# Attention stages tied in one order on the tensor engine, value products behind the transposes, and linear-attention products grouped by rows and columns

## The chip, the cores and the metric

The kernel runs on one core of a Trainium2 chip. The metric is the device time of one execution in microseconds (us), as a median of runs; a profiled execution gives the times of the single instructions. The engines are TensorE (PE in the rows, PEld for its weight loads), VectorE (DVE), ScalarE (ACT), GpSimd (POOL) and SyncE (SP), which issues most DMAs. Each engine runs its own list of instructions in the order in which the program was built, and waits at semaphores for the others.

## What is computed

One inference step of a two-layer diffusion backbone, on 512 latent tokens and 128 context tokens. Layer 0 mixes neighbourhood attention and a bidirectional gated linear attention, layer 1 is grouped-query attention; a convolutional feed-forward block follows each. Cut to what the change touches:

```
def block_attention(q, k, v):                 # layer 1, and context tokens of layer 0
    s = einsum('bhgqd,bhkd->bhgqk', qblk, k) * scale
    p = softmax(s, axis=-1)
    return einsum('bhgqk,bhkd->bhgqd', p, v)

def neighbourhood_attention(...):             # layer 0, latent tokens
    s_loc = q . k_window * scale + bias;  s_ctx = q . k_ctx * scale
    p = softmax(concat([s_loc, s_ctx], -1))
    o = p[..., :nk] . v_window + p[..., nk:] . v_ctx

def gla_scan(q, k, v, g, s0):                 # layer 0, linear attention, forward and backward
    o_inter = (q * exp(bcum)) . s             # from the running state
    att[i, j] = sum_d q[i,d] k[j,d] decay(i, j, d)
    o = o_inter + att . v
    s_new = exp(blast) * s + k_dec^T . v
```

## The kernel before, in words

Activations lie with features on the partitions and the 640 tokens (NT) along the free dimension, in two halves of 320. Projections split each operand into a high and a low part in float32r and take three matmuls per 128 x 128 block (`step`, L153); in the rows these are `mm`, each 128 rows by 128 columns of the array and 320 columns of moving data.

An attention is cut into units. A unit of layer 1 is one head and one block of 128 queries: its stage `scores` makes four matmuls into PSUM (`gs`, L1259 and L1260); `exps` takes the row maximum (L1011) and multiplies it by the scale (L1013) on VectorE, and the exponential with its row sum on ScalarE (L1017); `norm` takes the reciprocal of the sum (L1022) and scales the probabilities `gp` by it on VectorE (L1025); `turn` transposes these in five blocks of 128 on TensorE (`gpt`, L1268); `gather` copies them to SBUF (`gpy`, L1272 on VectorE, L1273 on ScalarE); `values` multiplies by the values for two heads at once (`gpo`, L1279: ten matmuls of 128 rows by 64 columns, the two heads in the two column halves). Layer 0's units have the same stages (`nas`, `nap`, `napt`, `napx`, `napo`), with a bias added to the scores. After each head pair comes a unit for the context tokens (`ctxs`, `ctxpt`, `ctxo`).

`pipeline` traces the stages of three successive units in turn: scores and exps of the newest, gather and values of the oldest, norm and turn of the middle one. Behind each stage it draws a few steps of other work (`fill.some(rate)`: in layer 1 the query projections of later heads and the first half of the output projection). Stages are traced at a higher priority (`AHEAD`) than the fill, and a scheduler then orders each engine's list at build time by priority and readiness. `tc.issue_after(ins)` makes what is traced under it follow `ins` on the same engine. In layer 1 (`paced`) the fill has to follow the last stage that returned an instruction, which is `scores` only, since no other stage returns one.

The linear attention (`gla_scores`, `gla_states`, `gla_out`) builds, for two head pairs m, products of 32 x 32 (`lev`, L860), of 32 and 64 columns (`off`, L881 and L884), and the outputs (`go`: the product with the values at L949 on all 128 rows, two products with the states, forward L951 and backward L952, on the 64 rows of one head). A matmul with float32 operands shows as two records in the trace; a transpose shows as one.

Of the kernel before, what the change touches and what calls it, by code (L numbers as in the profile page):

```python
# [18 lines left out]
LAT = 512  # L19
CTX = 128  # L20
NT = LAT + CTX
# [9 lines left out]
def kernel(ctx: ExitStack, tc: tile.TileContext, a: dict, o: dict):  # L31
    nc = tc.nc
# [799 lines left out]
    def gla_scores(m, k, q, F, G, fill):  # L832
# [38 lines left out]
        fill.some(ROFF, SOFF)  # L871
        big, small = PS("off"), PS("offx")
        res = {}
        for e in range(2):
            pe = slice(64 * e, 64 * e + 64)
            for t in range(5):
                dst = big[:, e, 128 * t:128 * t + 128] if t < 4 else small[:, e, 0:128]
                for j in range(4):
                    b = j // 2
                    s = slice(128 * t + 32 * j, 128 * t + 32 * j + 32)  # L880
                    nc.tensor.matmul(dst[32 * j:32 * j + 32, 64 * b:64 * b + 64], A32[pe, s],  # L881
                                     B32[pe, 128 * t + 64 * b:128 * t + 64 * b + 64], start=True, stop=True)
# [53 lines left out]
    def gla_out(m, q, F, G, vg, att, S, OT, fill):  # L936
        qd = []
        for c in (F, G):
            x = C("qd")
            last = expo(x[:, 0:NT], c[:, 0:NT])  # L940
            nc.gpsimd.tensor_tensor(x[:, 0:NT], x[:, 0:NT], q[:, 0:NT], ALU.mult)
            qd.append(x)
        for e, pe in col_pairs():
            h = 2 * m + e
            ps = PS("go")
            for t in range(5):
                dst = ps[:, 0, 128 * t:128 * t + 128] if t < 4 else ps[:, 1, 0:128]
                s = slice(128 * t, 128 * t + 128)
# [81 lines left out]
    def na_units(m, q, kk, kl, kch, kcl, vw, vc, vctx, ot):  # L1030
        units = []

        def unit(bp, e, mates):
# [20 lines left out]
            def turn():  # L1054
                u["pt"] = [P1("napt") for _ in range(2)]
                for i in range(2):
                    for t in range(3):
                        nc.tensor.transpose(u["pt"][i][:, 128 * t:128 * t + 128], u["p"][i][:, 128 * t:128 * t + 128], ident)

            def gather():  # L1060
                u["x"] = [T("napx", "napx", n=512, bufs=4) for _ in range(2)]
# [6 lines left out]
            def values():  # L1068
                po = P1("napo", "po")
                for i in range(2):  # L1070
                    b = 2 * bp + i
                    for t in range(3):
                        v = vw[b, t] if t < 2 else vc
                        for f in range(2):
                            hh = 2 * m + f
                            nc.tensor.matmul(po[64 * f:64 * f + 64, 128 * i:128 * i + 128], v[:, 64 * hh:64 * hh + 64],  # L1076
                                             mates[f]["x"][i][:, 128 * t:128 * t + 128], start=(t == 0), stop=(t == 2))
                dst = ot[:, 0:LAT].rearrange("p (r b i) -> p b r i", b=4, i=16)
                nc.scalar.copy(dst[:, 2 * bp:2 * bp + 2], po[:, 0:256].rearrange("p (b r i) -> p b r i", b=2, i=16))

            u.update(scores=scores, turn=turn, gather=gather)
            if e:
# [10 lines left out]
    def context_unit(q, kk, kl, ks, scale, vcol, ot):  # L1093
        u = {}

        def scores():
            ps = PS("ctxs")
            for e in range(2):
                dst = ps[:, e, 0:128]
                nc.tensor.matmul(dst, q[e][:, LAT:NT], kk[e][:, ks], start=True, stop=False)  # L1100
                nc.tensor.matmul(dst, q[e][:, LAT:NT], kl[e][:, ks], start=False, stop=True)
            u["s"] = ps[:, :, 0:128]

        def turn():
            u["pt"] = P1("ctxpt")
            for e in range(2):
                nc.tensor.transpose(u["pt"][:, 128 * e:128 * e + 128], u["p"][e], ident)

        def gather():
            u["x"] = T("ctxx", "ctxx", n=256, bufs=1)  # L1110
# [2 lines left out]
        def values():  # L1113
            po = P1("ctxo", "po")
            for e in range(2):
                nc.tensor.matmul(po[64 * e:64 * e + 64, 0:128], vcol(e), u["x"][:, 128 * e:128 * e + 128], start=True, stop=True)
            nc.scalar.copy(ot[:, LAT:NT], po[:, 0:128])

        def view():
            t = T("ctxp", "ctxp", n=256, bufs=2)  # L1120
# [32 lines left out]
    def layer1(xs, rs, mods):  # L1153
# [91 lines left out]
        def units_of(m, q, r):  # L1245
# [5 lines left out]
            def unit(b, e, mates):  # L1251
# [23 lines left out]
                def values():  # L1275
                    po = P1("gpo", "po")
                    for t in range(5):
                        for f in range(2):
                            nc.tensor.matmul(po[64 * f:64 * f + 64, 0:128], vs[t][:, 64 * kv:64 * kv + 64],  # L1279
                                             mates[f]["x"][:, 128 * t:128 * t + 128], start=(t == 0), stop=(t == 4))  # L1280
                    nc.scalar.copy(ot[:, s], po[:, 0:128])

                u.update(scores=scores, turn=turn, gather=gather)
                if e:
# [308 lines left out]
```

## Time and profile before

| | |
|---|---|
| median of 3 runs | 1748.98 us (1746.35 to 1754.0) |
| profiled execution: device time | 1748.81 us |
| profiled execution: span from the first to the last instruction | 1747.0 us |
| TensorE busy | 1672.7 us, 96% |
| VectorE busy | 1277.5 us, 73% |
| ScalarE busy | 722.8 us, 41% |
| chain that ended last: share of TensorE / VectorE / DMA | 81% / 12% / 3% |

How to read it: a busy TensorE is a union of spans whose ends are modelled, and matmuls overlap, so what an instruction costs is read from the distance between the starts of successive rows, not from its duration. The linear attention lies between 90 and 282 us, the neighbourhood attention to 420, the grouped-query attention between 983 and 1225; the rest is projections and the feed-forward blocks.

### The profile page before, as it was taken

To read this page: it belongs to the slowest core of one execution; us is meant where nothing else is said; L and a number is where in the kernel's file an instruction comes from. 1 tells how busy PE (TensorE), PEld (TensorE's weight loads), DVE (VectorE), ACT (ScalarE), POOL (GpSimd) and SP (SyncE) were. 2 spreads that over 40 slices of the span, in tenths; PEclk is the share of its full clock that TensorE was granted. 3 is DMA by queue.
4 is the path that set the end of the run, shared out by engine and by line. 5 is a ranking of instruction groups with operands and counts; after the bars stand their busy time and mean duration, and the time that the engine had idled before them with its cause. 6 is when DMAs were issued, how large, how long until landed. Compare 5 with 4: busy or idle time off the path is not lost.

```text
span 1747.0 us, 33431 instructions
## 1 busy us (share of the span) xinstructions
PE 1672.7 (96%) x13142; PEld 1573.8 (90%) x13142; DVE 1277.5 (73%) x2877; ACT 722.8 (41%) x1599; POOL 206.2 (12%) x475
## 2 busy tenths in 40 slices
PE   8978899989999999999999999999999999999997
PEld 6867777879899999999998788878899999999997
DVE  5899954765899989997557988875775644663654
ACT  4443254454533322332335566754453322331342
POOL 2134441310200000000003311000110000000001
PEclk8988998999999999999999999999999999999998
DMA  8623223233154555444232200110212222222222
GB/s 314 207 91 130 98 86 99 80 101 97 55 175 155 159 169 183 148 149 131 69 120 89 66 20 19 35 67 22 73 61 74 85 73 73 73 66 93 72 64 72
DMA packets 68014, 175.22 MB, mean 100 GB/s; under 512 B 7920, under 2 KB 9744, under 8 KB 66832
## 3 DMA queue, kind: packets, MB, share of 16 engines
q1 hardware_dynamic: 67024, 171.48, 30.2%
q8 instruction: 103, 1.69, 0.4%
q0 software_dynamic: 832, 1.60, 0.3%
q14 instruction: 55, 0.45, 0.1%
HBM read 165.71 MB, written 7.34 MB: 99 GB/s over the span
## 4 chain that ended last, share of the span: by engine, by line
PE 81%; DVE 12%; DMA 3%; ACT 2%; issue 2%; POOL 0%; SPq 0%; ACTq 0%; DVEq 0%; POOLq 0%
PE mm L153 65%; PE gpo L1279 3%; PE gpt L1268 2%; DVE junk L316 1%; DVE wa L316 1%; PE gs L1259 1%; DMA wa<-in_ada_wt_dram 1%; DVE wl L112 1%; PE gs L1260 1%; PE napo L1076 1%; DVE eb L847 1%; PE ss L410 1%; PE go L949 1%; DVE ea L841 1%; DMA x<-in_xT_dram 1%
## 5 line engine op out<-in xcount | busy, mean ns | idle before, releaser
L153 PE MATMUL mm<-hh,wl 128*128 128x320 f32 x2080 | 651.7, 315 | 5.3 <-DVE x L488 1.0
L153 PE MATMUL mm<-hl,wh 128*128 128x320 f32 x2080 | 648.4, 312 | 0.0
L153 PE MATMUL mm<-hh,wh 128*128 128x320 f32 x2080 | 642.0, 312 | 0.0
L111 ACT CAST wh<-ws 128x512 fp32r<-128x512 f32 x376 | 228.8, 615 | 443.0 <-PE mm L153 404.0
L153 PEld LDWEIGHTS mm<-hh,wl 128*128 128x128 f32 x2080 | 394.6, 190 | 15.6 <-issue 5.9
L153 PEld LDWEIGHTS mm<-hl,wh 128*128 128x128 f32 x2080 | 395.4, 190 | 2.9 <-DVE h L445 1.2
L153 PEld LDWEIGHTS mm<-hh,wh 128*128 128x128 f32 x2080 | 393.3, 190 | 0.9 <-issue 0.3
L112 DVE TENSOR_TENSOR wl<-ws,wh 128x512 fp32r<-128x512 f32 x348 | 240.2, 693 | 159.3 <-ACT wh L111 158.4
L153 PE MATMUL mm<-glo,wh 128*128 128x320 f32 x704 | 217.0, 309 | 0.0
L153 PE MATMUL mm<-ghi,wh 128*128 128x320 f32 x704 | 216.7, 309 | 0.0
L153 PE MATMUL mm<-ghi,wl 128*128 128x320 f32 x704 | 215.8, 309 | 0.0
L488 DVE SCALAR_TENSOR_TENSOR x<-mm,mod,x 128x192 f32<-128x192 f32 (+2 forms) x240 | 96.8, 435 | 93.4 <-PE mm L153 92.6
L153 PEld LDWEIGHTS mm<-ghi,wl 128*128 128x128 f32 x704 | 131.7, 188 | 0.9 <-issue 0.9
L153 PEld LDWEIGHTS mm<-glo,wh 128*128 128x128 f32 x704 | 132.2, 188 | 0.0
L153 PEld LDWEIGHTS mm<-ghi,wh 128*128 128x128 f32 x704 | 132.0, 188 | 0.1
L316 DVE SCALAR_TENSOR_TENSOR junk<-wa,sb 128x512 f32<-128x512 f32 x160 | 115.6, 727 | 7.5 <-DMA wa<-in_ada_wt_dram 7.2
L316 DVE SCALAR_TENSOR_TENSOR wa<-wa,sb 128x512 f32<-128x512 f32 x160 | 117.7, 742 | 0.3
L522 POOL MEMSET u<- 128x1 f32 x88 | 8.9, 103 | 766.3 <-DVE gate L515 432.3
L525 ACT COPY u<-mm 128x320 f32<-128x320 f32 x88 | 37.8, 432 | 88.0 <-PE mm L153 83.1
L592 PE MATMUL tm<-wl,hh 128*128 128x256 f32 x200 | 58.6, 297 | 9.8 <-ACT v L601 7.0
L1011 DVE TENSOR_REDUCE mx<-gs 128x1 f32<-128x640 f32 x64 | 52.5, 821 | 16.6 <-PE gs L1260 16.0
L1017 ACT ACTIVATE gp<-gs,mx,rq 128x640 f32<-128x640 f32 x64 | 57.1, 892 | 9.5 <-DVE mx L1013 5.1
(302 smaller groups left out, 2480.7 us busy)
## 6 DMA issues: line engine op xcount, KB each, us to landing
ws<-in_wu_dram SPq DMA_DIRECT2D x88, 512.0 KB, 3.2
wa<-in_ada_wt_dram SPq DMA_DIRECT2D x160, 256.0 KB, 3.3
ws<-in_wd_dram SPq DMA_DIRECT2D x32, 448.0 KB, 3.2
aw<-in_ada_w_dram SPq DMA_DIRECT2D x8, 1024.0 KB, 15.7
ws<-in_w_ab_dram SPq DMA_DIRECT2D x16, 512.0 KB, 4.2
ws<-in_wd_dram SPq DMA_DIRECT2D x16, 512.0 KB, 3.7
x<-in_xT_dram SPq DMA_DIRECT2D x16, 320.0 KB, 5.5
ws<-in_w_gqa_dram SPq DMA_DIRECT2D x10, 512.0 KB, 3.9
```

The costliest lines, as they stand in the source:

```text
L111: nc.scalar.copy(hi, src)
L112: eng.tensor_tensor(lo, src, hi, ALU.subtract)
L153: nc.tensor.matmul(ps, x, y[:, s], start=st, stop=sp_)
L316: nc.vector.scalar_tensor_tensor(w if v else junk, w, 1.0, cs[v, j], ALU.mult, ALU.mult, accum_out=acc[:, k, v, j:j + 1])
L410: nc.tensor.matmul(ps[0:rows, c:c + 2], part[:, t], onesd, start=True, stop=True)
L488: nc.vector.scalar_tensor_tensor(x[:, b:e], ps[:, b - HN * h:e - HN * h], gate[:, v, m:m + 1], old[:, b:e], ALU.mult, ALU.add)
L525: nc.scalar.copy(u[:, 1:321], ps)
L592: nc.tensor.matmul(ps, hh[:, s], wlo, start=(k == 0), stop=False)
L1011: nc.vector.tensor_reduce(mx[:, 0:n], s, axis, ALU.max, negate=True)
L1017: nc.scalar.activation(dst, src, AF.Exp, bias=mx[:, i:i + 1], accum_out=sm[:, i:i + 1], **kw)
L1268: nc.tensor.transpose(dst, u["p"][0][:, 128 * t:128 * t + 128], ident)
L1279: nc.tensor.matmul(po[64 * f:64 * f + 64, 0:128], vs[t][:, 64 * kv:64 * kv + 64], mates[f]["x"][:, 128 * t:128 * t + 128], start=(t == 0), ...
```

## The change

Four edits. `pipeline` puts `values` behind `norm` and `turn`, and makes each stage's TensorE instructions follow the last one of the stage before it (`behind_it`); every stage with TensorE work now returns its last instruction. The fill of layer 1 is paced by scores and values, not by turn. In `gla_scores` the `off` products of 32 columns all come before those of 64 columns. In `gla_out` the products with the values come first for the five token blocks, then the products with the states. Line numbers of the code behind the change are about 15 higher.

```diff
@@ gla_scores
-        for e in range(2):
-            pe = slice(64 * e, 64 * e + 64)
-            for t in range(5):
-                dst = big[:, e, 128 * t:128 * t + 128] if t < 4 else small[:, e, 0:128]
-                for j in range(4):
-                    ...
-                    nc.tensor.matmul(dst[32 * j:32 * j + 32, 64 * b:64 * b + 64], A32[pe, s],
+        blocks = [(e, slice(64 * e, 64 * e + 64), t, big[:, e, 128 * t:128 * t + 128] if t < 4 else small[:, e, 0:128])
+                  for e in range(2) for t in range(5)]
+        for width in (32, 64):
+            for e, pe, t, dst in blocks:
+                if width == 32:
+                    for j in range(4):
+                        ...
+                    continue
                 for b in range(2):
                     nc.tensor.matmul(dst[64 * b:64 * b + 64, 64 - 64 * b:128 - 64 * b],
@@ gla_out
             for t in range(5):
-                nc.tensor.matmul(dst, vg[t][:, 128 * h:128 * h + 128], att[m, e][:, s], start=True, stop=(t == 4))
-                if t < 4:
-                    nc.tensor.matmul(dst, S[m, 0][pe, t, :], qd[0][pe, s], start=False, stop=False)
-                    nc.tensor.matmul(dst, S[m, 1][pe, 3 - t, :], qd[1][pe, s], start=False, stop=True)
+                nc.tensor.matmul(dst[t], vg[t][:, 128 * h:128 * h + 128], att[m, e][:, cols[t]], start=(t in (0, 4)), stop=(t == 4), skip_group_check=True)
+            for t in range(4):
+                nc.tensor.matmul(dst[t], S[m, 0][pe, t, :], qd[0][pe, cols[t]], start=False, stop=False, skip_group_check=True)
+                nc.tensor.matmul(dst[t], S[m, 1][pe, 3 - t, :], qd[1][pe, cols[t]], start=False, stop=(t == 3), skip_group_check=True)
@@ pipeline
+        behind_it = None
...
-            for lag, stage in ((0, "scores"), (0, "exps"), (2, "gather"), (2, "values"), (1, "norm"), (1, "turn")):
+            for lag, stage in ((0, "scores"), (0, "exps"), (2, "gather"), (1, "norm"), (1, "turn"), (2, "values")):
                 if stage in window[lag]:
-                    with tc.high_priority(offset=AHEAD):
+                    with tc.high_priority(offset=AHEAD), ExitStack() as behind:
+                        if behind_it is not None:
+                            behind.enter_context(tc.issue_after(behind_it))
                         last = window[lag][stage]()
                     if last is not None:
-                        fill.after = last.ins
+                        behind_it = last.ins
+                        if stage != "turn":
+                            fill.after = last.ins
@@ turn, values of the three kinds of unit, scores of the context unit
-                        nc.tensor.transpose(dst, u["p"][0][:, 128 * t:128 * t + 128], ident)
+                        last = nc.tensor.transpose(dst, u["p"][0][:, 128 * t:128 * t + 128], ident)
+                    return last
```

In layer 1 of the program before, TensorE's list mixes transposes of one unit with value products of others; this piece is the one that ran from 1139.10 us.

```order
L1279 MATMUL gpo<-gpy,v 64x128
L1268 MATMUL gpt<-ident,gp 128x128 x2
L1279 MATMUL gpo<-gpy,v 64x128
L1268 MATMUL gpt<-ident,gp 128x128
L1279 MATMUL gpo<-gpy,v 64x128
L1268 MATMUL gpt<-ident,gp 128x128
L1279 MATMUL gpo<-gpy,v 64x128
L1268 MATMUL gpt<-ident,gp 128x128
L1279 MATMUL gpo<-gpy,v 64x128 x4
L1279 MATMUL gpo<-gpy,gvc 64x128 x2
L1259 MATMUL gs<-gkk,q 128x320
```

The same engine and layer in the changed program, an unbroken piece of its list, shows each stage whole.

```order
L1274 MATMUL gs<-gkl,q 128x320
L153 MATMUL mm<-hh,wl 128x320
L153 MATMUL mm<-hl,wh 128x320
L153 MATMUL mm<-hh,wh 128x320
L153 MATMUL mm<-hh,wl 128x320
L153 MATMUL mm<-hl,wh 128x320
L153 MATMUL mm<-hh,wh 128x320
L1282 MATMUL gpt<-ident,gp 128x128 x5
L1294 MATMUL gpo<-gpy,v 64x128 x8
L1294 MATMUL gpo<-gpy,gvc 64x128 x2
L1273 MATMUL gs<-gkk,q 128x320
```

The value products have moved together behind the five transposes; between the scores of a unit and the transposes of the unit before it stand six matmuls of fill here.

VectorE's list of the changed program at such a place, with buffer numbers: the maximum of one unit's scores (mx_13090), the normalisation that belongs to it (gp_13092), and between them the maximum of the next unit's scores (gs_13114).

```order
L1020 TENSOR_REDUCE mx_13090<-gs_13085 128x1
L1022 TENSOR_TENSOR mx_13090<-mx_13090,rq_10745 128x1
L1287 COPY gpy_13128<-gpt_13107 128x256
L112 TENSOR_TENSOR wl_13948<-ws_13945,wh_13947 128x512
L1020 TENSOR_REDUCE mx_13119<-gs_13114 128x1
L1031 RECIPROCAL sm_13091<-sm_13091 128x1
L1022 TENSOR_TENSOR mx_13119<-mx_13119,rq_10745 128x1
L1034 TENSOR_SCALAR gp_13092<-gp_13092,sm_13091 128x640
```

On TensorE the transposes of gp_13092 stand behind the scores gs_13114 and six matmuls of fill; so they come after the reduction of gs_13114 in any case.

Output products of the linear attention on TensorE, before:

```order
L949 MATMUL go<-att,v 128x128
L951 MATMUL go<-qd,S 128x128
L952 MATMUL go<-qd,S 128x128
L949 MATMUL go<-att,v 128x128
L951 MATMUL go<-qd,S 128x128
L952 MATMUL go<-qd,S 128x128
```

And in the changed program, the last head's piece:

```order
L955 MATMUL go<-qd,S 128x128
L954 MATMUL go<-qd,S 128x128
L955 MATMUL go<-qd,S 128x128
L954 MATMUL go<-qd,S 128x128
L955 MATMUL go<-qd,S 128x128 x2
```

The products with the states (64 rows) now follow each other, and those with the values (L952 of the changed kernel, 128 rows) stand in groups of up to ten ahead of them. Counted over TensorE's whole list, the shape of the array's tile (rows by columns) changes 520 times before and 289 times in the changed program: 127 and 62 times in the linear attention, 76 and 40 in the neighbourhood attention, 236 and 104 in the grouped-query attention. Within `off` it changes 34 and 2 times, within `go` 33 and 3 times.

## Rows read from the trace of the kernel before

**Rows 1.** The page, busy time of TensorE: us, share of the span, instructions.

```profile
PE 1672.7 (96%) x13142; PEld 1573.8 (90%) x13142; DVE 1277.5 (73%) x2877; ACT 722.8 (41%) x1599; POOL 206.2 (12%) x475
```

**Rows 2.** Busy time by stretch: stretch, length, PE, PEld, DVE, ACT, POOL, clock, DMA.

```profile
90.00:282.00 192.00, 162.44 (x2126) 143.93 (x2125) 155.02 (x306) 72.64 (x135) 76.09 (x56) 0.87 0.32 104
260.00:282.00 22.00, 22.00 (x142) 18.06 (x142) 6.11 (x15) 3.75 (x9) 3.85 (x6) 0.69 0.39 131
282.00:420.00 138.00, 127.14 (x1016) 110.48 (x1015) 92.17 (x193) 69.00 (x180) 23.92 (x38) 0.98 0.26 82
982.90:1225.50 242.60, 239.22 (x2103) 201.45 (x2101) 191.71 (x543) 148.39 (x353) 25.32 (x20) 1.00 0.11 36
```

**Rows 3.** TensorE in time, unmixed stages: start, length, what, count of records.

```profile
1049.32 0.38 PE L1268 MATMUL gpt<-ident,gp 128*128 128x128 f32 x2
1049.54 0.38 PE L1107 MATMUL ctxpt<-ident,ctxp 128*128 128x128 f32 x2
1049.85 1.09 PE L1279 MATMUL gpo<-gpy,v 128*64 128x128 f32 x16
...
1051.09 0.42 PE L1259 MATMUL gs<-gkk,q 128*128 128x320 f32 x1
```

**Rows 4.** TensorE in time, a mixed piece of the same layer.

```profile
1140.19 0.33 PE L1268 MATMUL gpt<-ident,gp 128*128 128x128 f32 x1
1140.45 0.43 PE L1279 MATMUL gpo<-gpy,v 128*64 128x128 f32 x2
1140.81 0.33 PE L1268 MATMUL gpt<-ident,gp 128*128 128x128 f32 x1
```

**Rows 5.** TensorE in time, scores and the fill behind them.

```profile
1053.65 0.31 PE L1260 MATMUL gs<-gkl,q 128*128 128x320 f32 x1
1053.80 0.31 PE L153 MATMUL mm<-hh,wl 128*128 128x320 f32 x1
```

**Rows 6.** VectorE in time, behind two scores; idle time and releaser in brackets.

```profile
1048.97 0.82 DVE L1011 TENSOR_REDUCE mx<-gs 128x1 f32<-128x640 f32 x1 [0.28 <-PE gs L1260]
...
1051.68 0.55 DVE L1025 TENSOR_SCALAR gp<-gp,sm 128x640 f32<-128x640 f32 x1
...
1054.00 0.82 DVE L1011 TENSOR_REDUCE mx<-gs 128x1 f32<-128x640 f32 x1 [0.20 <-PE gs L1260]
...
1054.93 0.55 DVE L1025 TENSOR_SCALAR gp<-gp,sm 128x640 f32<-128x640 f32 x1
```

**Rows 7.** VectorE and TensorE in time: a copy, and a transpose released by it.

```profile
1000.96 0.42 DVE L1272 COPY gpy<-gpt 128x256 f32<-128x256 f32 x1
1001.44 0.33 PE L1268 MATMUL gpt<-ident,gp 128*128 128x128 f32 x1 [0.44 <-DVE gpy L1272]
```

**Rows 8.** Waits of TensorE, 982.9 to 1225.5: who for whom, us, times, longest.

```profile
PE gpt L1268 <- DVE gpy L1272: 0.4, 1, 0.4
```

**Rows 9.** Waits of TensorE, 282 to 420.

```profile
PE napo L1076 <- ACT napx L1066: 2.9, 4, 2.2
```

**Rows 10.** TensorE in time, outputs of the linear attention.

```profile
245.19 0.49 PE L949 MATMUL go<-att,v 128*128 128x128 f32 x2
245.61 0.48 PE L951 MATMUL go<-qd,S 64*128 64x128 f32 x2
245.93 0.38 PE L952 MATMUL go<-qd,S 64*128 64x128 f32 x2
246.25 0.49 PE L949 MATMUL go<-att,v 128*128 128x128 f32 x2
```

**Rows 11.** TensorE in time, products of 32 and 64 columns.

```profile
230.72 0.33 PE L884 MATMUL off<-eb,ea 64*64 64x64 f32 x4
230.88 0.28 PE L884 MATMUL offx<-eb,ea 64*64 64x64 f32 x4
231.09 0.32 PE L881 MATMUL off<-eb,ea 64*32 64x64 f32 x8
231.34 0.33 PE L884 MATMUL off<-eb,ea 64*64 64x64 f32 x4
```

More of the change, by code (lines that the diff above doesn't have):

```diff
@@ L873, in gla_scores @@
         res = {}
-        for e in range(2):
-            pe = slice(64 * e, 64 * e + 64)
-            for t in range(5):
-                dst = big[:, e, 128 * t:128 * t + 128] if t < 4 else small[:, e, 0:128]
-                for j in range(4):
-                    b = j // 2
-                    s = slice(128 * t + 32 * j, 128 * t + 32 * j + 32)
-                    nc.tensor.matmul(dst[32 * j:32 * j + 32, 64 * b:64 * b + 64], A32[pe, s],
-                                     B32[pe, 128 * t + 64 * b:128 * t + 64 * b + 64], start=True, stop=True)
+        blocks = [(e, slice(64 * e, 64 * e + 64), t, big[:, e, 128 * t:128 * t + 128] if t < 4 else small[:, e, 0:128])
[4 more added lines that the diff above has]
+                    for j in range(4):
+                        b = j // 2
+                        s = slice(128 * t + 32 * j, 128 * t + 32 * j + 32)
+                        nc.tensor.matmul(dst[32 * j:32 * j + 32, 64 * b:64 * b + 64], A32[pe, s],
+                                         B32[pe, 128 * t + 64 * b:128 * t + 64 * b + 64], start=True, stop=True)
+                    continue
                 for b in range(2):
@@ L945, in gla_out @@
             ps = PS("go")
+            dst = [ps[:, 0, 128 * t:128 * t + 128] if t < 4 else ps[:, 1, 0:128] for t in range(5)]
+            cols = [slice(128 * t, 128 * t + 128) for t in range(5)]
             for t in range(5):
-                dst = ps[:, 0, 128 * t:128 * t + 128] if t < 4 else ps[:, 1, 0:128]
-                s = slice(128 * t, 128 * t + 128)
-                nc.tensor.matmul(dst, vg[t][:, 128 * h:128 * h + 128], att[m, e][:, s], start=True, stop=(t == 4))
-                if t < 4:
-                    nc.tensor.matmul(dst, S[m, 0][pe, t, :], qd[0][pe, s], start=False, stop=False)
-                    nc.tensor.matmul(dst, S[m, 1][pe, 3 - t, :], qd[1][pe, s], start=False, stop=True)
+                nc.tensor.matmul(dst[t], vg[t][:, 128 * h:128 * h + 128], att[m, e][:, cols[t]], start=(t in (0, 4)), stop=(t == 4), skip_group_check=True)
+            for t in range(4):
+                nc.tensor.matmul(dst[t], S[m, 0][pe, t, :], qd[0][pe, cols[t]], start=False, stop=False, skip_group_check=True)
+                nc.tensor.matmul(dst[t], S[m, 1][pe, 3 - t, :], qd[1][pe, cols[t]], start=False, stop=(t == 3), skip_group_check=True)
             fill.some(ROUT)
@@ L1057, in turn @@
                     for t in range(3):
-                        nc.tensor.transpose(u["pt"][i][:, 128 * t:128 * t + 128], u["p"][i][:, 128 * t:128 * t + 128], ident)
+                        last = nc.tensor.transpose(u["pt"][i][:, 128 * t:128 * t + 128], u["p"][i][:, 128 * t:128 * t + 128], ident)
+                return last
             def gather():
@@ L1075, in values @@
                             hh = 2 * m + f
-                            nc.tensor.matmul(po[64 * f:64 * f + 64, 128 * i:128 * i + 128], v[:, 64 * hh:64 * hh + 64],
-                                             mates[f]["x"][i][:, 128 * t:128 * t + 128], start=(t == 0), stop=(t == 2))
+                            last = nc.tensor.matmul(po[64 * f:64 * f + 64, 128 * i:128 * i + 128], v[:, 64 * hh:64 * hh + 64],
+                                                    mates[f]["x"][i][:, 128 * t:128 * t + 128], start=(t == 0), stop=(t == 2))
                 dst = ot[:, 0:LAT].rearrange("p (r b i) -> p b r i", b=4, i=16)
                 nc.scalar.copy(dst[:, 2 * bp:2 * bp + 2], po[:, 0:256].rearrange("p (b r i) -> p b r i", b=2, i=16))
+                return last
             u.update(scores=scores, turn=turn, gather=gather)
@@ L1100, in scores @@
                 nc.tensor.matmul(dst, q[e][:, LAT:NT], kk[e][:, ks], start=True, stop=False)
-                nc.tensor.matmul(dst, q[e][:, LAT:NT], kl[e][:, ks], start=False, stop=True)
+                last = nc.tensor.matmul(dst, q[e][:, LAT:NT], kl[e][:, ks], start=False, stop=True)
             u["s"] = ps[:, :, 0:128]
+            return last
         def turn():
@@ L1106, in turn @@
             for e in range(2):
-                nc.tensor.transpose(u["pt"][:, 128 * e:128 * e + 128], u["p"][e], ident)
+                last = nc.tensor.transpose(u["pt"][:, 128 * e:128 * e + 128], u["p"][e], ident)
+            return last
         def gather():
@@ L1115, in values @@
             for e in range(2):
-                nc.tensor.matmul(po[64 * e:64 * e + 64, 0:128], vcol(e), u["x"][:, 128 * e:128 * e + 128], start=True, stop=True)
+                last = nc.tensor.matmul(po[64 * e:64 * e + 64, 0:128], vcol(e), u["x"][:, 128 * e:128 * e + 128], start=True, stop=True)
             nc.scalar.copy(ot[:, LAT:NT], po[:, 0:128])
+            return last
         def view():
@@ L1267, in turn @@
                         dst = u["pt"][0][:, 128 * t:128 * t + 128] if t < 2 else u["pt"][1][:, 128 * (t - 2):128 * (t - 2) + 128]
-                        nc.tensor.transpose(dst, u["p"][0][:, 128 * t:128 * t + 128], ident)
+                        last = nc.tensor.transpose(dst, u["p"][0][:, 128 * t:128 * t + 128], ident)
+                    return last
                 def gather():
@@ L1278, in values @@
                         for f in range(2):
-                            nc.tensor.matmul(po[64 * f:64 * f + 64, 0:128], vs[t][:, 64 * kv:64 * kv + 64],
-                                             mates[f]["x"][:, 128 * t:128 * t + 128], start=(t == 0), stop=(t == 4))
+                            last = nc.tensor.matmul(po[64 * f:64 * f + 64, 0:128], vs[t][:, 64 * kv:64 * kv + 64],
+                                                    mates[f]["x"][:, 128 * t:128 * t + 128], start=(t == 0), stop=(t == 4))
                     nc.scalar.copy(ot[:, s], po[:, 0:128])
+                    return last
                 u.update(scores=scores, turn=turn, gather=gather)
```

## The prediction

> **What bounds the kernel now.** I read the busy line of the page first: TensorE works 1672.7 us of a span of 1747.0 us, 96%; VectorE is next with 73% [rows 1]. So anything that shortens TensorE's list should show, unless another engine is close behind. The stretches say where that could be [rows 2]. In the grouped-query attention (982.9 to 1225.5 us) TensorE is busy 239.2 of 242.6 us and VectorE 191.7 (79%); in the linear attention (90 to 282 us) TensorE has 162.4 of 192.0 us and VectorE 155.0 (81%), so there TensorE is not alone in setting the pace; in the neighbourhood attention VectorE has 92.2 of 138.0 us. The page's busy time is a union of modelled spans, so I price TensorE's instructions by the distance between starts.
>
> The waits come next. The longest of TensorE at a transpose of the grouped-query stage is 0.4 us, once [rows 8]: the old order never made it wait for the softmax. In the neighbourhood attention it waited 2.9 us for copies of transposed probabilities [rows 9].
>
> **Price of a change of tile shape.** The change removes and adds no arithmetic. The count of matmuls and DMAs stays, and the other engines do the same work in nearly the same order. Some 30 fill matmuls move from the grouped-query stage to behind it, which costs the same there. What falls is the number of places at which the array's tile shape changes: 520 to 289. In an unmixed stage two transposes take 0.22 us, 0.11 each; two transposes followed by a value product take 0.31 us, so the entry into 128 x 64 costs 0.09 us, and the whole value stage of 20 records takes 1051.09 - 1049.85 = 1.24 us, 0.062 a record with its exit [rows 3]. In a mixed piece one transpose and one value product of two records take 1140.81 - 1140.19 = 0.62 us [rows 4]; unmixed they are 0.11 + 2 x 0.062 = 0.234. So 0.386 us go to two changes, 0.19 each. The bounds are 0.09 and 0.19; most of the changes that go are of the mixed kind, but parts of a stage were already whole, so I take 0.15 us.
>
> **Grouped-query attention, shape changes.** They fall from 236 to 104, by 132: 132 x 0.15 = 20 us gained (12 to 25 by the bounds).
>
> **Grouped-query attention, new wait.** The turn now stands behind the scores of the next unit and, mostly, six fill matmuls, and the value products that used to be mixed into the transposes stand behind them, so these cover nothing any more. On VectorE the changed list has, in 31 of some 70 turns (64 of query units, the rest of context units), the maximum of the next unit's scores ahead of the normalisation that the turn needs. The trace of before has this sequence: the last score starts at 1053.65 and the matmul behind it at 1053.80 [rows 5]; the maximum starts at 1054.00 and the normalisation ends at 1054.93 + 0.55 = 1055.48 [rows 6]; a transpose starts 0.06 us after the VectorE instruction that releases it ends (1001.38 to 1001.44) [rows 7]. So the transposes can start 1055.48 + 0.06 - 1053.80 = 1.74 us after the scores leave TensorE. A fill matmul lasts as long as a score, 0.15 us [rows 5], six of them 0.90: the wait is 0.84 us. Of the 31 turns four have three fill matmuls between (1.29 us each), nineteen have six (0.84), four have nine (0.39), and four have more (none): 5.2 + 16.0 + 1.6 = 23 us lost. In the other turns the normalisation comes first; its own chain from maximum to end takes 1052.23 - 1048.97 = 3.26 us [rows 6], and TensorE has the rest of the previous unit's stages and its own scores and fill, over 4 us, to cover it: nothing. The ends for this term are 0, if VectorE runs ahead of the list's worst reading, and 64 x 0.84 = 54 us, if every turn of a query unit meets that wait. What is queued behind a waiting transpose is all of TensorE's list, value products included; who waits for TensorE then is VectorE with its next maximum, so a wait does not catch up later. The 0.4 us of before goes.
>
> The Trainium skill bears on this ("TensorE: Matmul & The Clock Gate", section "Step-by-step: what each phase is for"): the matmuls themselves stay in program order, only weight loads are pulled ahead. By that rule the value products behind a waiting transpose cannot fill its gap, which is the sum above; were they free to, the 23 us would vanish and the sum be rival B's. The transpose at 1001.44, which idled 0.44 us with value products of another unit on the list, agrees with the rule as far as one wait can.
>
> **Neighbourhood attention.** 36 changes go: 36 x 0.15 = 5.4 us (3.2 to 6.8). The value products now come behind the next turn, so the copies that they wait for have longer: I take 2 of the 2.9 us [rows 9] as gone. A turn may wait for its normalisation here too, but VectorE has a third of the stretch free; ±4 us. Together 7.4 us gained.
>
> **Linear attention, off.** A group of 32-column products takes 0.25 us before the next 64-column one starts, a 64-column one 0.16 with its own shape behind it [rows 11]: 0.09 of a change, again up to 0.19. Of the 32 changes that go, half belong to the first pair of heads, where VectorE and the loading of activations set the pace; I count the 16 of the second pair, at 0.09 to 0.19: 2 us gained (1.4 to 3; 6 if all 32 count).
>
> **Linear attention, go.** One token block of one head takes 246.25 - 245.19 = 1.06 us: 0.42 for the value product, 0.32 for each product with a state [rows 10]. There are 16 such blocks with states. Grouped, the value product has its own shape before and behind it; a transpose of the same 128 x 128 x 128 takes 0.11 a record, so two records 0.22 instead of 0.42, 0.2 less: 16 x 0.21 = 3.4 us gained. The product with the backward state starts 0.32 us behind the forward one already without a change of shape, so I leave state products at 0.32. If they too fell to 0.22, it would be 6.7 us.
>
> Here the trace and the Trainium skill stand together against the grouping ("TensorE: Matmul & The Clock Gate", section "The mechanism"): a weight load overlaps matmuls in flight only where its row group differs. Eight state products in succession use the same 64 rows, so by the rule each waits for the one ahead; the 0.32 us of the second one agrees. By the rule the term is 3.4 us, without it 6.7.
>
> The end of this stage, 260 to 282 us, ran with a granted clock of 0.69, a mean between its two levels of 1.2 and 2.4 GHz [rows 2]. TensorE was busy throughout it; denser work elsewhere could shift that stretch. I take it as unchanged, ±4 us.
>
> **The sum.** -20 (shape changes) + 23 (waits) - 0.4 (old wait) - 7.4 (neighbourhood) - 2 (off) - 3.4 (go) = -10.2 us. Against the profiled execution's 1748.81 us that is 1738.6; the median of the runs is 0.2 us higher, 1748.98, so 1739.
>
> **The rivals.** A is the forecast. Its own range is 1726 to 1749, from the shape price (±8) and a wait of 15 to 31 us.
>
> B: the waits stay mostly hidden, 8 us or less, since VectorE, released earlier by shorter TensorE stages, has the normalisation done before the scores of the next unit finish. For it: over half of the turns have that order on the list already, and VectorE has 21% of the stage free. Against it: in the other 31 the list forbids it. 1748.8 - 33.2 + 8 = 1724.
>
> C, slower: every turn meets the 0.84 us wait, because each wait of TensorE delays the next scores, so that the next maximum also comes late. 54 us instead of 23: 1748.8 - 33.2 + 54 = 1770. It decides for slower once the waits pass 33 + 9 = 42 us. For it: the value products no longer cover the turn, and VectorE at 79% has little to catch up with. Against it: more than half of the turns have the normalisation ahead of that maximum.
>
> D, no change: the shape price is nearer 0.09 and the gains of the linear and neighbourhood attentions are absorbed by VectorE (155 of 192 us busy in the first), so that 12 us of shape changes and the old waits meet 12 to 16 us of new waits: 1748. That the shapes are not changed as told is not a rival, since the lists show it; that they cost nothing by themselves, and the mixed piece is long for another reason, ends near 1765 with C.
>
> **How the numbers follow.** A 0.46, B 0.22, C 0.14, D 0.18. What a measurement of this kernel can tell from no change is 0.5%, 8.7 us: faster is below 1740, slower above 1757.7. A lies on both sides of 1740: I give 0.29 of its 0.46 to faster and 0.16 to same, with 0.01 to slower. B is faster, C slower, D same. Faster 0.51, same 0.34, slower 0.15. The range reaches to B's 1724 with its spread and into C: 1718 to 1764. A's own stands above.
>
> **What would show it.** In the grouped-query stage TensorE should wait for the normalised probabilities some 31 times, 0.8 us each; near zero speaks for B, over 40 us for C. Its length should be 242.6 - 20 + 23 = 245 us (±8). The value stage should be 1.24 us wherever it stands. The go blocks should go from 1.06 to 0.85 us, and the neighbourhood attention become some 7 us shorter. The forecast fails if a whole stage does not save 0.15 us per change, or if the scores come so late that VectorE, and no more TensorE, sets the length of the stage.

## The result, and the profile after

The changed kernel takes 1762.92 us (median of 6 runs, 1760.19 to 1765.78) against 1747.86 us before: ratio 1.0086, 95% interval 1.0063 to 1.0108. It is slower by some 15 us; 1739 us were predicted. Its profiled execution has a span of 1760.9 us, against 1747.0.

The page's busy line and the chain of waits, after:

```profile
PE 1642.4 (93%) x13142; PEld 1571.5 (89%) x13142; DVE 1287.7 (73%) x2877; ACT 724.6 (41%) x1599; POOL 207.5 (12%) x475
...
PE 76%; DVE 17%; DMA 2%; ACT 2%; issue 2%; POOL 0%; SPq 0%; ACTq 0%; DVEq 0%; POOLq 0%
```

TensorE is busy 30 us less than before [rows 1] with the same instructions, and yet the end is 14 us later: it now idles. VectorE's share of the chain went from 12% to 17%.

Where it happened is read from the first score of each attention and from the last product of the context units (profiled executions, us):

| | before | after |
|---|---|---|
| neighbourhood attention, first score | 279.5 | 264.4 |
| grouped-query attention, first score | 982.9 | 967.4 |
| its last context product | 1225.5 | 1237.1 |
| its length | 242.6 | 269.7 |
| end of the span | 1747.0 | 1760.9 |

The kernel arrives at the grouped-query attention 15.5 us early and loses 27.1 there. Busy time of that stage (columns as in rows 2), after:

```profile
967.40:1237.60 270.20, 227.89 (x2075) 202.60 (x2074) 200.51 (x537) 149.99 (x352) 24.78 (x20) 0.94 0.10 31
```

TensorE's busy time in it fell by 11 us [rows 2], some 4 of them since 28 records of fill are no longer in it; it idles 42 us where it idled 3; and the granted clock, 1.00 before, is 0.94. Between the levels 1.2 and 2.4 GHz that is about 12% of the stage, 32 us, at the lower one. The groups of TensorE there (busy us and mean ns, then idle time before them by what ended it), after:

```profile
L1282 PE MATMUL gpt<-ident,gp 128*128 128x128 f32 x320 | 49.9, 289 | 30.5 <-DVE gp L1034 12.3 <-DVE rq L1239 5.4 <-DVE ny L349 5.1
...
L1294 PE MATMUL gpo<-gpy,v 128*64 128x128 f32 x512 | 40.2, 306 | 4.6 <-DVE nx L341 4.6
```

The transposes waited 0.4 us before [rows 8] and 30.5 now. Several releasers are named, but they are all VectorE instructions beside the normalisation `gp` in its list, and the one that the transposes need is that normalisation. An ordinary case, late in the stage, TensorE and then VectorE in time:

```profile
1215.54 0.31 PE L1274 MATMUL gs<-gkl,q 128*128 128x320 f32 x1
1215.68 0.31 PE L153 MATMUL mm<-hh,wl 128*128 128x320 f32 x1
...
1216.42 0.31 PE L153 MATMUL mm<-hh,wh 128*128 128x320 f32 x1
1217.32 0.74 PE L1282 MATMUL gpt<-ident,gp 128*128 128x128 f32 x5 [0.59 <-DVE mx L1022]
```

```profile
1214.60 0.68 DVE L112 TENSOR_TENSOR wl<-ws,wh 128x512 fp32r<-128x512 f32 x1
1215.72 0.16 DVE L1031 RECIPROCAL sm<-sm 128x1 f32<-128x1 f32 x1 [0.44 <-ACT gp L1026]
1215.88 0.82 DVE L1020 TENSOR_REDUCE mx<-gs 128x1 f32<-128x640 f32 x1
1216.63 0.55 DVE L1034 TENSOR_SCALAR gp<-gp,sm 128x640 f32<-128x640 f32 x1
1217.09 0.15 DVE L1022 TENSOR_TENSOR mx<-mx,rq 128x1 f32<-128x1 f32 x1
```

This is the predicted sequence: scores, six fill matmuls, and on VectorE the maximum of these scores ahead of the normalisation that the transposes need. The last fill starts at 1216.42 and the transposes at 1217.32: 0.90 us between starts, of which 0.15 is the fill itself, so 0.75 us of wait (0.84 predicted). But other cases look like this, TensorE and VectorE:

```profile
1123.41 0.31 PE L153 MATMUL mm<-hh,wh 128*128 128x320 f32 x1
1126.46 1.30 PE L1282 MATMUL gpt<-ident,gp 128*128 128x128 f32 x5 [2.74 <-DVE ny L349]
1127.69 0.48 PE L1294 MATMUL gpo<-gpy,v 128*64 128x128 f32 x2
```

```profile
1121.81 0.73 DVE L1193 STREAM_SHUFFLE gy<-gx 128x512 f32<-128x512 f32 x1
1122.44 0.81 DVE L1020 TENSOR_REDUCE mx<-gs 128x1 f32<-128x640 f32 x1
1123.17 1.35 DVE L112 TENSOR_TENSOR wl<-ws,wh 128x512 fp32r<-128x512 f32 x1
1124.44 0.15 DVE L341 TENSOR_SCALAR nx<-gst 128x10 f32<-128x10 f32 x1
1124.52 1.13 DVE L1022 TENSOR_TENSOR mx<-mx,rq 128x1 f32<-128x1 f32 x1
1125.58 0.15 DVE L1031 RECIPROCAL sm<-sm 128x1 f32<-128x1 f32 x1
...
1125.77 0.55 DVE L1034 TENSOR_SCALAR gp<-gp,sm 128x640 f32<-128x640 f32 x1
```

Here a later query head's preparation (`gy`, `nx`) and a weight split (`wl`) stand in the list too; the wait is 2.9 us, and the value products behind it (1127.69) do not fill it, although the copies that they read had ended by 1122.9.

Taken over all 64 turns of query units (distance from the matmul ahead, less 0.15 us), 23 waited, 34.2 us together: sixteen 1.0 us on average, seven over 2 us, 18.2 us together. Each of the 23 starts 0.15 us after its own normalisation ends, and 22 of them have the next maximum ahead of that normalisation. The transposes of the context units add 4.0 us. The other 41 turns hardly waited.

### The profile page after: what moved, and what is told of

Same layout as the page of the kernel before. It is cut to its first block, busy times and chain, and to the rows that moved or that the text cites. A ratio compares the mean times of both kernels' runs of the same rounds, so it can differ in the third digit from the quotient of the medians.

```text
span 1760.9 us, 33502 instructions
## 1 busy us (share of the span) xinstructions
PE 1642.4 (93%) x13142; PEld 1571.5 (89%) x13142; DVE 1287.7 (73%) x2877; ACT 724.6 (41%) x1599; POOL 207.5 (12%) x475
## 4 chain that ended last, share of the span: by engine, by line
PE 76%; DVE 17%; DMA 2%; ACT 2%; issue 2%; POOL 0%; SPq 0%; ACTq 0%; DVEq 0%; POOLq 0%
PE mm L153 63%; PE gpo L1294 2%; DVE mx L1020 2%; PE gpt L1282 2%; DVE junk L316 2%; DVE wl L112 2%; DVE wa L316 2%; PE gs L1273 1%; PE ss L410 1%; PE gs L1274 1%; DVE eb L847 1%; DMA wa<-in_ada_wt_dram 1%; DVE gp L1034 1%; DVE q L613 1%; PE napo L1086 1%
## 5 line engine op out<-in xcount | busy, mean ns | idle before, releaser
L488 DVE SCALAR_TENSOR_TENSOR x<-mm,mod,x 128x192 f32<-128x192 f32 (+2 forms) x240 | 96.6, 435 | 83.8 <-PE mm L153 82.7
L316 DVE SCALAR_TENSOR_TENSOR wa<-wa,sb 128x512 f32<-128x512 f32 x160 | 113.4, 715 | 0.2
L1282 PE MATMUL gpt<-ident,gp 128*128 128x128 f32 x320 | 49.9, 289 | 30.5 <-DVE gp L1034 12.3
L1282 PEld LDWEIGHTS gpt<-ident,gp 128*128 128x128 f32 x320 | 39.4, 148 | 36.4 <-issue 18.0
```

What stands on the lines that cost most here:

```text
L316: nc.vector.scalar_tensor_tensor(w if v else junk, w, 1.0, cs[v, j], ALU.mult, ALU.mult, accum_out=acc[:, k, v, j:j + 1])
L488: nc.vector.scalar_tensor_tensor(x[:, b:e], ps[:, b - HN * h:e - HN * h], gate[:, v, m:m + 1], old[:, b:e], ALU.mult, ALU.add)
L1282: last = nc.tensor.transpose(dst, u["p"][0][:, 128 * t:128 * t + 128], ident)
```

## The experiments

Times are medians; the kernel before, run beside them, took 1749.3 to 1750.0 us, against 1747.86 beside the changed kernel, so a difference between an experiment and the changed kernel is open by some 2 us. Ratios are to the kernel before. In the edits `...` marks lines left out.

**Which part gains, which loses.** In `e1_gla_only` and `e8_off_only` the pipeline is the old one.

> Only the linear attention is changed (off by widths, go by products); the pipeline of attention units is the old one. Theory S (the grouped products themselves save the time that the changed kernel gains ahead of the neighbourhood attention, whose first score starts at 264.4 instead of 279.5 us): that start falls by 10 to 16 us and the time by as much, to 1732 to 1738 us. Rival L (the 15 us came from another pattern of the granted clock in that one profile): the start moves by under 5 us and the time lies within 5 us of the kernel before.

> The kernel before with only the off products grouped by width; go as before. The two groupings together gave 7.6 us. The prediction's terms (off 2, go 3.4): 1746 to 1748 us. If off carries it: 1741 to 1743 us. If off gives nothing (VectorE and the activations set the pace there): 1749 us, and go gives the whole 7.6.

Measured: off alone 1743.87 us, ratio 0.9977 (0.9963 to 0.9991); off and go 1741.82 us, ratio 0.9956 (0.9944 to 0.9968). So off is worth about 4 us and go about 3.7, as far as the intervals tell. The first expectation missed: the first score of the neighbourhood attention did move, to 263.8 us, but only half of those 15 us reach the end (in that profile 8.9). The go blocks after:

```profile
234.96 2.39 PE L952 MATMUL go<-att,v 128*128 128x128 f32 x20
237.29 0.49 PE L954 MATMUL go<-qd,S 64*128 64x128 f32 x4
...
239.84 0.38 PE L954 MATMUL go<-qd,S 64*128 64x128 f32 x2
240.07 0.38 PE L955 MATMUL go<-qd,S 64*128 64x128 f32 x2
240.29 0.38 PE L954 MATMUL go<-qd,S 64*128 64x128 f32 x2
```

Ten value products take 2.33 us, 0.23 each, and a state product starts 0.22 us after the one before: 0.23 + 2 x 0.22 = 0.67 us a block instead of 1.06 [rows 10].

The other half of the split: all of the change, but the grouped-query stage as before.

```diff
+        order = ((0, "scores"), (0, "exps"), (2, "gather"), (1, "norm"), (1, "turn"), (2, "values"))
+        if paced:
+            order = ((0, "scores"), (0, "exps"), (2, "gather"), (2, "values"), (1, "norm"), (1, "turn"))
...
-                        if behind_it is not None:
+                        if behind_it is not None and not paced:
...
-                        if stage != "turn":
+                        if stage == "scores" and "ctx" not in window[lag] if paced else stage != "turn":
```

> All of the change except in grouped-query attention, where stages are ordered and paced as before (values ahead of norm and turn, no tie). Theory W (the whole loss lies in the grouped-query stage, in turns that wait for VectorE): the stage is 243 us (plus or minus 4) at a full granted clock, the time 1763 - 27 = 1736 us (1731 to 1742). If the tie in the neighbourhood attention also loses, the time is 4 to 8 us above that of the kernel with the linear attention alone; if it gains by its 36 shape changes, 5 us below.

Measured 1735.62 us, ratio 0.9916 (0.9903 to 0.9929). The whole loss lies in the grouped-query stage, 1762.92 - 1735.62 = 27.3 us (29.7 by the ratios), and the tie in the neighbourhood attention gains (1741.82 to 1735.62 us). That stage is as long as before, at the full clock:

```profile
972.10:1215.10 243.00, 239.70 (x2105) 201.77 (x2104) 192.21 (x544) 148.66 (x354) 25.34 (x20) 1.00 0.11 36
```

**Is it the order on VectorE?** The theory so far: take the next maximum out of the normalisation's way, and the waits go.

```diff
-            for lag, stage in ((0, "scores"), (0, "exps"), (2, "gather"), (1, "norm"), (1, "turn"), (2, "values")):
+            for lag, stage in ((0, "scores"), (1, "norm"), (0, "exps"), (2, "gather"), (1, "turn"), (2, "values")):
...
+                        if stage == "exps" and normed is not None:
+                            behind.enter_context(tc.issue_after(normed))
...
+                    if stage == "norm":
+                        normed, last = last.ins, None
```

> The changed kernel with one more tie, on VectorE: the maximum of a unit's scores follows the normalisation of the unit before (0 of 64 turns have the next maximum ahead of their normalisation, against 23). TensorE's order of stages is that of the changed kernel. Theory W (turns wait because the next maximum stands ahead): most of the 34 us in front of turns go and the granted clock of the stage returns to 0.98 or more, time 1763 - 30 - 8 = 1725 us (1718 to 1738). Rival R (the fixed order on TensorE costs it): 1755 to 1768 us, waits of the turns merely move to other instructions.

Measured 1766.42 us, ratio 1.0090 (1.0077 to 1.0104): nothing gained. The theory fell: no turn has the next maximum ahead of it now, and 34 wait, 41 us together by the same distances. The waits of that kernel's transposes in the stage (who for whom, us, times, longest) are more, not fewer:

```profile
PE gpt L1287 <- DVE gp L1038: 35.5, 30, 3.1
```

TensorE and VectorE in time show why:

```profile
1213.27 0.31 PE L1279 MATMUL gs<-gkl,q 128*128 128x320 f32 x1
1213.41 0.31 PE L153 MATMUL mm<-hh,wl 128*128 128x320 f32 x1
...
1216.26 0.31 PE L153 MATMUL mm<-hh,wh 128*128 128x320 f32 x1
1217.76 0.74 PE L1287 MATMUL gpt<-ident,gp 128*128 128x128 f32 x5 [1.20 <-DVE gp L1038]
```

```profile
1213.65 0.55 DVE L1038 TENSOR_SCALAR gp<-gp,sm 128x640 f32<-128x640 f32 x1
1214.12 0.82 DVE L1024 TENSOR_REDUCE mx<-gs 128x1 f32<-128x640 f32 x1
...
1216.51 0.16 DVE L1035 RECIPROCAL sm<-sm 128x1 f32<-128x1 f32 x1 [1.18 <-ACT gp L1030]
1216.60 0.55 DVE L488 SCALAR_TENSOR_TENSOR x<-mm,mod,x 128x320 f32<-128x320 f32 x1
1217.07 0.54 DVE L1038 TENSOR_SCALAR gp<-gp,sm 128x640 f32<-128x640 f32 x1
```

The scores end at 1213.41. Until the transposes of the same unit TensorE has 1216.26 + 0.15 - 1213.41 = 3.0 us of work: fill, the previous turn, the next scores, fill. The softmax takes from 1214.12 to 1217.61, 3.5 us, and began 0.7 us late behind the previous normalisation. Some 0.4 us of the 3.5 is a residual update (`x`, L488) that stands before the normalisation; what is left, begun late, still does not fit. Where a softmax of this profile is as short as its cover, 2.9 us each, the transposes still wait 0.4 us (the turn at 1223.63), for the late start. So neither of these two orders on VectorE hides the softmax; they choose which turn waits, and what else VectorE has to do lengthens the wait.

**Is it the distance?** So the tie's fault would be that it holds the turn one unit behind its scores. Before, the transposes were free to slip: for units 50 to 62 in the trace of before they start 3.8 to 9.2 us after their normalisation ends. Two units behind, tie kept (`late` is 1 in the grouped-query stage):

```diff
+        late = 1 if paced else 0
...
-            for lag, stage in ((0, "scores"), (0, "exps"), (2, "gather"), (1, "norm"), (1, "turn"), (2, "values")):
+            for lag, stage in ((0, "scores"), (0, "exps"), (2 + late, "gather"), (1 + late, "norm"), (1 + late, "turn"), (2 + late, "values")):
```

> The changed kernel, and in grouped-query attention norm and turn belong to the unit two (not one) behind the newest scores, gather and values to the one three behind. The tie stays, the shapes stay whole. Theory D (distance: the tie pins the turn one unit behind its scores, where TensorE has 3.2 to 4.4 us of work, and the softmax of one unit takes 3.3 us plus whatever VectorE has ahead of each step): with a second unit between, the turns wait under 8 us in all, the granted clock of the stage returns to 0.98 or more, the stage takes 222 to 236 us and the time is 1715 to 1732 us. Rival V (VectorE itself cannot keep the pace of the tied order): waits of 25 us or more remain, time 1750 us or more.

Measured 1721.74 us, ratio 0.9841 (0.9824 to 0.9858): the fastest kernel of this study, 1.6% faster than before. The stage takes 229.9 us:

```profile
969.00:1199.40 230.40, 214.80 (x2078) 192.40 (x2077) 195.04 (x538) 146.53 (x351) 24.61 (x20) 0.99 0.11 37
```

and its transposes (columns as for the groups above):

```profile
L1283 PE MATMUL gpt<-ident,gp 128*128 128x128 f32 x320 | 49.3, 275 | 5.6 <-DVE gpy L1288 3.2 <-ACT gpy L1289 1.3 <-DVE gp L1035 0.9
```

The normalisation ends 0.9 us of waits instead of most of 30.5, although 38 turns now have the next maximum ahead of it on VectorE. By distances between starts six turns wait, 3.7 us together. VectorE has the same work in 40 us less, so it was not the bound (rival V). Some waits are left: 5.6 us at transposes and 6.9 at value products.

Is that gain the whole shapes or the distance alone? The same without the tie in this stage (`if behind_it is not None and not paced:`):

> The kernel with the second unit between scores and turn, without the tie in grouped-query attention: transposes and value products mix again. It tells whether the gain of that kernel (1721.7 us) comes from whole shapes or from the larger distance alone. If whole shapes, once no turn waits, are worth what was worked out (some 13 to 20 us): 1734 to 1742 us, stage 240 to 246 us. If the distance alone gives it: 1718 to 1727 us.

1739.18 us, ratio 0.9942 (0.9921 to 0.9962). The tie at distance two is worth 17.4 us. The stage without it:

```profile
969.60:1215.40 245.80, 239.39 (x2077) 198.31 (x2076) 192.94 (x538) 148.29 (x351) 24.81 (x20) 1.00 0.11 34
```

With the same number of fill matmuls TensorE is busy 239.39 - 214.80 = 24.6 us less under the tie; 9 us of that come back as idle time (15.6 us against 6.4). And the changed kernel without the tie, by the same line:

> The changed kernel without the tie in grouped-query attention: stages are traced in the new order (values behind norm and turn, fill paced by scores and values), but the scheduler may place transposes and value products as it likes. Theory D: the scheduler lets the turns slip behind again, the waits go (under 8 us), shapes are mixed again: stage 238 to 248 us, time 1731 to 1742 us, as with the old pipeline there. Rival O (the new order of the stages costs the time, not the tie): 1750 us or more.

1741.59 us, ratio 0.9966 (0.9951 to 0.9981): 21 us faster than with the tie, the waits at its transposes 2.8 us. At distance one the tie costs 21 us, at two it gains 17. It stays 6 us above the kernel with the old order there: its stage idles 9.7 of 249.9 us where that one idles 3.3 of 243.0. What in the new order makes that idle time was not separated.

**More work in between.** Three more ways to give the turn time. Value products ahead of norm and turn, at distance one and at two (the order of the two stages exchanged, as it was before):

> The changed kernel with the tie kept, but the value products traced ahead of norm and turn. Shapes stay whole. VectorE's list has the next maximum ahead of the normalisation in 27 turns of query units (23 in the changed kernel). Theory W: the 1.24 us of value products now stand between scores and turn in every second unit and cover that much, so of some 37 us of waits about half goes: 1740 to 1752 us. Rival R (a fixed order by itself costs the time, since the scheduler can no longer fill gaps): no gain, 1758 to 1768 us.

> The kernel with the second unit between scores and turn, tie kept, but value products traced ahead of norm and turn, which puts 1.24 us more of TensorE's work between scores and turn. Theory D (only distance matters): the turns hardly wait at the larger distance already, so nothing more is gained, 1718 to 1726 us. If the value products' place matters by itself, as it seemed at the short distance (1748.6 against 1762.9 us): 1708 to 1716 us.

At distance one 1748.55 us, 14 us less than the changed kernel (17 by the ratios), with 27 turns behind a next maximum but only 15.9 us of waits in them. At distance two 1727.09 us, 5 us more than with the values behind: where little cover is lacking, that place gains nothing.

More fill (`RGQA = 0.55` for 0.4):

> The changed kernel with the fill drawn at 0.55 steps a stage instead of 0.4, so some two matmuls more stand between the scores of a unit and the turn behind them (0.15 us each). Theory D: each waiting turn waits 0.3 to 0.4 us less, 10 to 15 us over the 31 waiting turns as long as the fill lasts, and some of the lower clock goes: 1745 to 1756 us. Rival (what stands in between is nothing to the wait, VectorE's own list sets the pace): 1760 to 1766 us.

1763.66 us: missed. The waits of the turns that have a next maximum ahead fell by 10 us, but the fill ran out (units 33 to 38 have none behind their scores) and the clock was no better. The stage is 277 us long, as it holds 63 more fill matmuls (some 9 us), and TensorE idles 39 us in it, against 42. So more fill in some turns left less for others and hardly changed the idle time.

**What the lower clock costs.** Idle products put into the measured gaps of the 23 turns (`IDLE` has their number for each unit, 143 in all):

```diff
+                    for _ in range(IDLE.get(8 * m + 2 * b + e, 0)):
+                        nc.tensor.matmul(u["pt"][1][:, 384:512], ident, ident, start=True, stop=True)
```

> The changed kernel with 143 idle products (128 x 128 x 128, float32, into an unused piece of the turn's PSUM tile; they compute nothing that is used) ahead of the 23 turns that waited, as many as fit into each turn's measured gap (some 31 us in all). Theory C (the waits also cost by the granted clock, which stood at its lower level for 34 us of the stage): the time at the lower level falls below 10 us and the whole gets faster although 31 us of work were added, 1750 to 1757 us. Rival N (the lower clock falls into the waits and costs nothing): 1763 us or up to 12 us more, where the idle products overrun a gap.

1756.87 us (1756.15 to 1759.42), ratio 1.0055 (1.0041 to 1.0068): 143 x 0.22 = 31.5 us of useless work were added and the kernel got 5 to 6 us faster than the changed one. The intervals of the two ratios just touch, so the sign is better known than the size. The stage has a clock of 0.99:

```profile
969.50:1234.40 264.90, 248.25 (x2361) 226.42 (x2360) 200.55 (x537) 149.69 (x352) 24.89 (x20) 0.99 0.10 32
```

The products stand in the waits: TensorE idles 17 us instead of 42. What is gone is time at the lower clock, by the mean from some 32 us to some 5. In the changed kernel it looks like this:

```profile
1140.00:1150.00 10.00, 7.50 (x64) 6.41 (x63) 9.39 (x23) 7.97 (x18) 0.00 (x0) 1.00 0.25 78
1150.00:1160.00 10.00, 8.61 (x82) 7.36 (x82) 7.71 (x23) 3.74 (x9) 2.77 (x2) 0.50 0.23 75
```

TensorE was busy 7.5 of 10 us in the first stretch, and ran at 1.2 GHz in the next.

## Why the prediction was wrong

- **What bounds the kernel, and where the waits come.** Right: the loss is in the grouped-query stage, at the transposes, for the normalisation, behind the next maximum. 23 query turns and five transposes of context units waited, where 31 of some 70 were read from the list. The stage took 270 us where 245 were predicted.
- **Price of a change of shape.** Right in size: 132 changes for 20 us were predicted. The tie at distance two takes 140 changes out of the trace of the stage (247 to 107) and 24.6 us of TensorE's busy time, 0.18 each, of which 17.4 us reach the end. But part of this is no change of shape, and the prediction put all of it into one price. In a whole value stage sixteen records start within 1050.78 - 1049.85 = 0.93 us:

```profile
1049.85 1.09 PE L1279 MATMUL gpo<-gpy,v 128*64 128x128 f32 x16
1050.78 0.39 PE L1279 MATMUL gpo<-gpy,gvc 128*64 128x128 f32 x4
```

That is 0.058 each, half the 0.11 of a transpose: record by record, the products of the two heads, in the two column halves, start in pairs 0.006 us apart. Between transposes a product of one head often has no partner, and its two records start 0.16 us apart. Of the 640 records 488 start in pairs before and in the untied kernel at distance two, 636 in the tied one. As an estimate from these counts the unpaired ones cost 76 x 0.11 = 8 us; no run separates this from the changes of shape.

- **Neighbourhood attention, off, go.** 7.4, 2 and 3.4 us predicted, about 6, 4 and 3.7 measured. From its second score (280.2 and 270.4 us) to its last context product (411.9 and 396.4) the neighbourhood attention went from 131.7 to 126.0 us; from the first score it stayed at 132, as that one score now starts 6 us ahead of the others. The go blocks fell by 0.39 us each in the trace (6.2 us over 16), nearer to the prediction's other end: the state products went to 0.22 us in succession. The prediction left them at 0.32 because the second one had no change of shape before it; it read merged rows. Record by record, before:

```profile
245.82 0.27 PE L951 MATMUL go<-qd,S 64*128 64x128 f32 x1
245.93 0.27 PE L952 MATMUL go<-qd,S 64*128 64x128 f32 x1
...
246.05 0.27 PE L952 MATMUL go<-qd,S 64*128 64x128 f32 x1
```

The first product starts at 245.61 [rows 10] and its own second record 0.21 us later, right behind the change of shape; the records after that follow at 0.11, and 0.20 us pass before the value product at 246.25 changes the shape back. So the 0.32 of before was the change of shape. By the rule of the Trainium skill ("TensorE: Matmul & The Clock Gate", section "The mechanism") that weight loads overlap matmuls in flight only across different row groups, products on the same rows would wait for each other; the trace does not show that, as they start every 0.22 us on the same 64 rows. The stretch from 260 to 282 us, taken as unchanged, ran at a clock of 0.92 instead of 0.69; what that gave at the end was not separated.

- **The step that failed: the new wait, 23 us.** It was sized on one clean piece of the trace, the maximum alone between scores and normalisation. The ordinary wait is near that: sixteen of 1.0 us on average. But seven waits of 2.6 us, where VectorE has other work in the list (2.7 to 4.4 us of it between maximum and normalisation in six of them, ahead of the maximum in the seventh), are 18 of the 34 us, and nothing in the sum allowed for them. With the context units it is 38 us for 23. "Over 4 us" of cover for a turn was wrong as well: in the ordinary case it is 3.0 us without value products between, 4.2 with. Without them it is less than the softmax takes with its late start, and this, not the place of the maximum alone, makes the wait: with norm first the turns waited no less, at distance two they hardly waited.
- **What the sum did not have: the clock.** No term stood for TensorE's clock in a stage that begins to idle. Filling the gaps gave back 5 to 6 us. The forecast missed by 25 us (-10.2 predicted, +15.1 measured): 15 are the waits, these 5 to 6 the clock; the rest is not separated.
- **The rivals.** The time lies nearer to that of C, 1770 us, than to the forecast, but by another mechanism: not every turn waits 0.84 us, a third of them wait more. Its deciding point, 42 us of waits, was about reached: 1762.92 - 1721.74 = 41.2 us is what distance two takes away, waits and clock together. B (8 us of waits or less) fell. That the time lies inside the stated range, 1718 to 1764, is luck: the forecast gave slower 0.15.

The books: -27.8 us is what the change gives at distance two (ratio 0.9841); +41.2 us is the price of distance one; 13.4 against 15 us measured. Both numbers come from the same run, so they split the loss in two and do not check it.

## What to carry to other kernels

A fixed order across stages trades the scheduler's freedom for whole shapes; before fixing it, compare the dependent chain (here 2.9 to 3.5 us of softmax on two engines, begun 0.2 to 0.7 us late) with the work that the fixed order leaves between its ends (here 3.0 us), and add a unit of distance if it does not fit. Price a wait over all its occurrences, with everything that stands in the other engine's list, not from the cleanest one. When the busy engine starts to idle, look at its granted clock too.

## What the runs showed of the hardware

A change between 128 and 64 rows of the array costs TensorE some 0.2 us each way with the same data (go blocks, 1.06 to 0.67 us for two changes); between 128 and 64 columns the entry alone costs 0.09 us [rows 3]. Successive float32 products on the same 64 rows start every 0.22 us, as on all 128 rows (0.23). Products of 64 columns in the two column halves start in pairs 0.006 us apart, so that a record takes 0.058 us on average instead of 0.11, when nothing stands between them. And useless work in TensorE's gaps made the kernel faster (1762.92 to 1756.87 us), while the stage's clock rose from 0.94 to 0.99.
